# A decoder layer: the second feed-forward's down projection with the activation as stationary operand, and its end with tokens on partitions

## The chip, the core and the metric

The kernel runs on one core of a Trainium2 chip. The metric is the device time of one execution in microseconds, the median of the runs. The engines have the names of the profile: PE (TensorE, products), PEld (its weight loads), DVE (VectorE), ACT (ScalarE), POOL (GpSimd) and SP (SyncE, which issues most DMAs here).

## The reference, cut to what matters

256 tokens with 2048 features get 16 meta tokens in front (272 in all), go through a feed-forward, a mixer (attention beside a short convolution, merged by gates) and a second feed-forward, and a last norm; the meta tokens are dropped. All is float32.

```python
D_MODEL, SEQ, N_META, D_FF = 2048, 256, 16, 5632

def rms_norm(x, g):
    y = x * lax.rsqrt(jnp.mean(x * x, axis=-1, keepdims=True) + RMS_EPS)
    return y * g

def swiglu_ffn(h, w_gu, w_down):
    gate, up = jnp.split(h @ w_gu, 2, axis=-1)
    return (jax.nn.silu(gate) * up) @ w_down

s = jnp.concatenate([meta, x], axis=1)
s = s + 0.5 * swiglu_ffn(rms_norm(s, norm_ffn1), ffn1_w_gu, ffn1_w_down)
...
s = s + merged @ w_out
s = s + 0.5 * swiglu_ffn(rms_norm(s, norm_ffn2), ffn2_w_gu, ffn2_w_down)
s = rms_norm(s, norm_final)
return s[:, N_META:]
```

## The kernel before, in words

The residual stream `s` is kept with features on partitions: `[128, 16 chunks, 272 tokens]`, L142. Every matrix product keeps float32 accuracy by splitting both operands in a high part and a low rest, both of the type float32r (`wh` and `wl` of the weights; the two parts of an activation lie side by side in a tile of class `Act`). A product is then the sum of three: high by high, high weights by low activation, low weights by high activation.

`linear` (L215) makes all the large products. For four output chunks of 128 features it takes four banks of PSUM and goes over the chunks of the contraction. The stationary operand (the one that is loaded into the array) is a 128x128 block of the weights, the moving one the activation with tokens along the row. Where only the 256 real tokens are computed, both parts of the activation fit one bank: `wh` is multiplied with both at once, 512 columns wide (L248), then `wl` with the high part, 256 wide (L252). With 272 tokens, or where `nj` is 1, it is three products of 272 or 256 columns (L250, L251, L252). Weights come in loads of 1 MB into `st` (four buffers, SP's queue), ScalarE casts a block to `wh` (L241), VectorE makes `wl` of it (L242), three buffers each.

Order of the work: what follows a group of outputs (its "evict") waits in the list `pending` and is put in behind the second chunk of the group after it (`EVICT_AT`). Small other work stands in the list `side`; `linear` puts one piece behind the chunks 5, 9 and 13. The framework's planner then orders each engine's instructions and hands out the slots of the pools. The pool `act` has `N_ACT` slots of 4352 bytes per partition, which tiles of several stages share (`xin`, `h1` to `h3`, `m`, `yo` and others).

A feed-forward (`ffn`, L276) is done in two halves of the hidden features, 24 and then 20 chunks: gate and up products, their elementwise part into the activation `m`, and then the down product of that half, which adds to `s` (L313). In the second feed-forward's last half, `after2` (L614) also squares the finished chunk and sums the squares over chunks, multiplies by the last norm's gain, and puts `turn_out` (L631) in `side`: two transposes on TensorE (L635) that turn a chunk to tokens on partitions and two copies into `yo`. The last four output chunks are done one at a time (`nj` = 1, `cut_last`). Behind the last product the sums of squares are turned by products with ones (L624), a root, a reciprocal and a Newton step (`rsqrt`, L203 to L208) give the factor `fr` for each token, `yo` is scaled in five pieces by VectorE and ScalarE (L655, L653), and SP issues five DMAs (L656).

Of the kernel before, what the change touches and what calls it, by code (L numbers as in the profile page):

```python
# [15 lines left out]
P = 128  # L16
D = 2048
# [17 lines left out]
N_ACT = 21  # L35
EVICT_AT = 1
WARM = 6


@with_exitstack  # L40
def decoder_layer(ctx: ExitStack, tc: tile.TileContext, t, out):
# [17 lines left out]
    # the tensor engine's clock comes up while the first loads are under way  # L59
# [21 lines left out]
    NV = 3 * DC + 3 * NH + 1  # L81
    vrows = const.tile([NV, P], F32, name="vrows")
    G_MIX, G_FFN2, G_FIN, G_CONV, G_SUB = 0, DC, 2 * DC, 3 * DC, NV - 1
# [6 lines left out]
    load_gain(G_FIN, t["norm_final"])  # L90
# [68 lines left out]
    def split(act, g, src):  # L159
        """A group's four chunks from float32."""  # L160
        for k in range(2):
            tl, f = act.tiles[2 * g + k], src[:, 2 * k : 2 * k + 2, :]
            nc.scalar.copy(out=tl[:, :, 0, :], in_=f)
            nc.vector.tensor_sub(tl[:, :, 1, :], f, tl[:, :, 0, :].bitcast(F32))

    def gain_split(h, c, gain):
        """gain * s for chunk c, split; the norm's factor for each token is left to the product's outputs."""
        w = h.width
        hi, lo = h.part(c, 0, 0, w), h.part(c, 1, 0, w)
        a = nc.scalar.mul(hi, s[:, c, T - w :], gain)  # L170
        b = nc.vector.scalar_tensor_tensor(
            out=lo, in0=s[:, c, T - w :], scalar=gain, in1=hi.bitcast(F32), op0=ALU.mult, op1=ALU.subtract
        )
        return a.ins, b.ins

    class Norm:
        """Sums of squares over the features, chunk by chunk, and 1 / rms for each token on every partition."""
# [4 lines left out]
        def add(self, c):  # L182
# [4 lines left out]
            nc.scalar.activation(sq[:, self.n0 :], s[:, c, self.n0 :], AF.Square)  # L187
# [12 lines left out]
    def rsqrt(out_, ms, shape, name):  # L200
        """1 / sqrt(ms) with a Newton step."""
# [8 lines left out]
    # ---- the linears: one stream of products; what follows a group of outputs, and any other work, is put  # L210
    # between the products of the groups after it ----
# [3 lines left out]
    def linear(act, chunks, w, k0, c0, t0, t1, name, evict, before=None, side_at=(5, 9, 13), nj=GC):  # L215
# [4 lines left out]
        kb = KB * GC // nj  # L220
        nl = kb if before is not None else LB * kb
        acc = [bank(f"{name}_{j}") for j in range(nj)]
        for b in range(0, len(chunks), kb):
            blk = chunks[b : b + kb]
            r0 = (k0 + blk[0]) * P
            wh = wpool.tile([P, kb, nj * P], F32R, tag="wh", name="wh")
            wl = wpool.tile([P, kb, nj * P], F32R, tag="wl", name="wl")
            m = len(blk)
            if b % nl == 0:
                st = wpool.tile([P, LB * kb, nj * P], F32, tag="st", bufs=ST_BUFS, name="st")  # L230
# [3 lines left out]
                    in_=w[r0 : r0 + ml * P, c0 : c0 + nj * P].rearrange("(c p) f -> p c f", p=P),  # L234
# [8 lines left out]
            for i, c in enumerate(blk):  # L243
                first, last = b + i == 0, b + i == len(chunks) - 1
                for j in range(nj):
                    a, f = acc[j][:, :n], slice(j * P, (j + 1) * P)
                    if shared(n, nj):
# [12 lines left out]
    def shared(n, nj):  # L260
        return 2 * n <= 512 and nj == GC

    def total(ps, n):
        """A product's sum, where its parts have accumulated side by side."""
# [11 lines left out]
    def ffn(h, w_gu, w_down, norm, n0, after, before=None, cut_last=False):  # L276
        """s += 0.5 * swiglu; `after(c)` once chunk c of s is done."""
        n = T - n0
        ng = F // GW
        halves = [list(range(0, (ng + 1) // 2)), list(range((ng + 1) // 2, ng))]  # L280
        allk = list(range(DC))
        for half in halves:
            m = Act("m", len(half) * GC, n)
            for gi, g in enumerate(half):
                sg = wide([P, GC, T], "sg")

                def gate(pg, sg=sg):
                    rstd = norm.rstd[:, n0:]
                    for j in range(GC):
                        gt = tmp.tile([P, T], F32, tag="gt", name="gt")  # L290
                        nc.vector.tensor_mul(gt[:, :n], total(pg[j], n), rstd)
                        sgm = tmp.tile([P, T], F32, tag="sgm", name="sgm")
                        nc.scalar.activation(sgm[:, :n], gt[:, :n], AF.Sigmoid)
                        nc.vector.tensor_mul(gt[:, :n], gt[:, :n], rstd)
                        nc.vector.tensor_mul(sg[:, j, :n], gt[:, :n], sgm[:, :n])

                def up(pu, sg=sg, gi=gi):
                    for j in range(GC):
                        nc.vector.tensor_mul(sg[:, j, :n], total(pu[j], n), sg[:, j, :n])
                    split(m, gi, sg[:, :, :n])  # L300

                linear(h, allk, w_gu, 0, g * GW, 0, n, "pg", gate, before=before)
                before = None
                linear(h, allk, w_gu, 0, F + g * GW, 0, n, "pu", up)
            final = half is halves[-1]
            c = 0
            while c < DC:
                nj = 1 if final and cut_last and c >= DC - GC else GC

                def down(pd, c=c):  # L310
                    for j in range(len(pd)):
                        for k in range(2 if shared(n, len(pd)) else 1):
                            nc.vector.scalar_tensor_tensor(  # L313
                                out=s[:, c + j, n0:], in0=pd[j][:, k * n : (k + 1) * n], scalar=0.5,
                                in1=s[:, c + j, n0:], op0=ALU.mult, op1=ALU.add,
                            )
                        if final:
                            after(c + j)

                linear(m, list(range(len(half) * GC)), w_down, half[0] * GC, c * P, 0, n, "pd", down, nj=nj)  # L320
                c += nj

# [4 lines left out]
    def prep(c):  # L327
# [5 lines left out]
        v = nc.vector.tensor_copy(s[:, c, :], pt[:, :T])  # L333
# [39 lines left out]
    ffn(h1, t["ffn1_w_gu"][0], t["ffn1_w_down"][0], norm1, 0, after1, before=before1)  # L373

# [48 lines left out]
    class Unit:  # L423
        """The attention of one head and one block of 128 queries, in three steps."""
# [106 lines left out]
    # the short convolution  # L531
# [33 lines left out]
    # gates, branches, merge  # L565
# [27 lines left out]
    norm3 = Norm(NMETA, "3")  # L593
    for d in range(D // GW):

        def o_evict(ps, d=d):
            for j in range(GC):
                c = d * GC + j
                for k in range(2):
                    nc.vector.tensor_add(s[:, c, NMETA:], ps[j][:, k * SEQ : (k + 1) * SEQ], s[:, c, NMETA:])  # L600
# [8 lines left out]
    yo = [[apool.tile([P, W2], F32, tag="act", name=f"yo{i}{q}") for q in range(2)] for i in range(2)]  # L609
    norm4 = Norm(NMETA, "4")  # L610

    fsum = []

    def after2(c):  # L614
        sc = s[:, c, NMETA:]
        if c < DC - 1:
            norm4.add(c)
        else:
            sq = tmp.tile([P, SEQ], F32, tag="half", name="fsq")
            nc.scalar.activation(sq, sc, AF.Square)  # L620
            for i in range(2):
                pr = bank(f"pr{i}")
                for k, q in enumerate((norm4.ssq[:, NMETA:], sq)):
                    nc.tensor.matmul(  # L624
                        pr[:, :1], q[:, i * P : (i + 1) * P], ones[:, 0:1], start=k == 0, stop=k == 1
                    )
                fsum.append(pr)
        nc.scalar.mul(sc, sc, col(G_FIN + c))
        side.append(lambda: turn_out(c))

    def turn_out(c):  # L631
        pt = bank("ot")
        c0 = c % NH * P
        for i in range(2):
# [47 lines left out]
```

## Time and profile before

| | before |
|---|---|
| median of 3 runs | 2238.79 us (2238.0 to 2239.01) |
| profiled execution, first to last instruction | 2236.7 us |
| median of the runs less that span | 2.1 us |
| PE, DVE, ACT busy | 2221.1, 1344.9, 1012.5 us |
| mean granted TensorE clock | 0.998 |
| read from HBM | 396.67 MB |
| weights of the down projections | 87 loads of 1 MB and 4 of 256 KB, 5.3 and 2.8 us to landing |

The page gives one execution's span; the runs' times stand beside it, and the profiled execution has no other time of its own. Rows of the timeline read: start, length, engine, line, operation, tile written <- tiles read, and shapes. Groups read: count, then busy us and mean ns of one, then idle time before it with its releaser. TensorE's products overlap their neighbours, so their cost is read from the distance of their starts and not from their lengths.

### The profile page before, as it was taken

The numbers are of one execution on the slowest core, as the hardware profiler recorded it, in microseconds if no ns is written. First come the engines' busy times: TensorE is split into PE (matmuls) and PEld (weight loads), VectorE is DVE, ScalarE is ACT, GpSimd is POOL, SyncE is SP. The second block draws the span as 40 slices with busy tenths as digits, with TensorE's granted clock in tenths as the row PEclk, the third lists the DMA queues.
The fourth block names the chain that finished last, engine by engine and source line by source line (L and its number), as shares of the span: only waits on it lengthen the run. The fifth ranks groups of instructions, "written<-read, shape, count | busy, mean of one in ns | idle before, by whom it ended". The sixth has DMA issues, their size and how long they took to land.

```text
span 2236.7 us, 35912 instructions
## 1 busy us (share of the span) xinstructions
PE 2221.1 (99%) x15068; PEld 2060.5 (92%) x15068; DVE 1344.9 (60%) x1978; ACT 1012.5 (45%) x1357; POOL 5.8 (0%) x16
## 2 busy tenths in 40 slices
PE   9999999999999999999999999999999999999998
PEld 8999999999999999898988888888888888888887
DVE  7555554455555565667766665776666655666665
ACT  6444333334434443445455454555444433545444
POOL 1000000000000000000000000000000000000000
PEclk9999999999999999999999999999999999999999
DMA  6554555555555555444565555555555555555553
GB/s 232 175 182 171 171 178 180 170 173 182 173 170 176 182 170 179 155 139 151 167 191 188 189 187 190 183 193 188 189 190 190 191 192 193 192 188 189 188 174 109
DMA packets 208738, 401.09 MB, mean 179 GB/s; under 512 B 6548, under 2 KB 16992, under 8 KB 208576
## 3 DMA queue, kind: packets, MB, share of 16 engines
q1 hardware_dynamic: 208192, 398.48, 53.7%
q8 instruction: 118, 1.93, 0.4%
q14 instruction: 44, 0.36, 0.0%
q0 software_dynamic: 288, 0.17, 0.0%
q10 hardware_dynamic: 96, 0.14, 0.0%
HBM read 396.67 MB, written 2.10 MB: 178 GB/s over the span
## 4 chain that ended last, share of the span: by engine, by line
PE 99%; ACT 0%; DMA 0%; DVE 0%; ACTq 0%; issue 0%
PE pg L252 8%; PE pd L252 8%; PE pu L252 8%; PE pu L248 7%; PE pg L248 7%; PE pd L248 6%; PE g L248 5%; PE pd L250 4%; PE pd L251 4%; PE pg L250 4%; PE pu L250 4%; PE pg L251 4%; PE pu L251 4%; PE g L252 3%; PE z L248 3%; PE o L248 3%
## 5 line engine op out<-in xcount | busy, mean ns | idle before, releaser
L242 DVE TENSOR_TENSOR wl<-st,wh 128x1024 fp32r<-128x1024 f32 (+1 forms) x754 | 919.7, 1222 | 803.3 <-ACT wh L241 802.4
L241 ACT CAST wh<-st 128x1024 fp32r<-128x1024 f32 (+1 forms) x754 | 792.0, 1051 | 1091.4 <-PE pd L251 155.5
L252 PE MATMUL pd<-m,wl 128*128 128x272 f32 (+1 forms) x1408 | 398.8, 283 | 0.0
L252 PE MATMUL pu<-h,wl 128*128 128x272 f32 (+1 forms) x1408 | 398.0, 283 | 0.0
L252 PE MATMUL pg<-h,wl 128*128 128x272 f32 (+1 forms) x1408 | 396.1, 284 | 0.0
L252 PEld LDWEIGHTS pd<-m,wl 128*128 128x128 f32 x1408 | 265.0, 188 | 0.0
L252 PEld LDWEIGHTS pu<-h,wl 128*128 128x128 f32 x1408 | 264.6, 188 | 0.0
L252 PEld LDWEIGHTS pg<-h,wl 128*128 128x128 f32 x1408 | 264.1, 188 | 0.3 <-DVE wl L242 0.2
L248 PE MATMUL pg<-h,wh 128*128 128x512 f32 x704 | 244.8, 394 | 0.0
L248 PE MATMUL pu<-h,wh 128*128 128x512 f32 x704 | 244.5, 394 | 0.0
L250 PE MATMUL pd<-m,wh 128*128 128x272 f32 (+1 forms) x784 | 226.3, 289 | 0.0
L251 PE MATMUL pd<-m,wh 128*128 128x272 f32 (+1 forms) x784 | 225.0, 287 | 0.0
L248 PE MATMUL pd<-m,wh 128*128 128x512 f32 x624 | 217.6, 395 | 0.0
L250 PE MATMUL pg<-h,wh 128*128 128x272 f32 x704 | 203.4, 290 | 2.0 <-ACT wh L241 2.0
L250 PE MATMUL pu<-h,wh 128*128 128x272 f32 x704 | 203.2, 289 | 0.0
L251 PE MATMUL pu<-h,wh 128*128 128x272 f32 x704 | 202.4, 288 | 0.0
L251 PE MATMUL pg<-h,wh 128*128 128x272 f32 x704 | 202.4, 288 | 0.0
L248 PE MATMUL g<-h,wh 128*128 128x512 f32 x512 | 180.1, 395 | 0.0
L248 PEld LDWEIGHTS pu<-h,wh 128*128 128x128 f32 x704 | 132.0, 188 | 30.7
L248 PEld LDWEIGHTS pg<-h,wh 128*128 128x128 f32 x704 | 132.0, 187 | 30.6
L251 PEld LDWEIGHTS pd<-m,wh 128*128 128x128 f32 x784 | 148.1, 189 | 0.0
L250 PEld LDWEIGHTS pd<-m,wh 128*128 128x128 f32 x784 | 147.5, 188 | 0.0
(211 smaller groups left out, 3336.9 us busy)
## 6 DMA issues: line engine op xcount, KB each, us to landing
st<-in_ffn_w_gu_dram SPq DMA_DIRECT2D x172, 1024.0 KB, 4.9
st<-in_ffn_w_down_dram SPq DMA_DIRECT2D x87, 1024.0 KB, 5.3
st<-in_w_in_dram SPq DMA_DIRECT2D x48, 1024.0 KB, 5.1
st<-in_w_gate_dram SPq DMA_DIRECT2D x32, 1024.0 KB, 5.7
st<-in_w_branch_dram SPq DMA_DIRECT2D x16, 1024.0 KB, 5.3
st<-in_w_out_dram SPq DMA_DIRECT2D x16, 1024.0 KB, 5.3
st<-in_ffn_w_gu_dram SPq DMA_DIRECT2D x8, 512.0 KB, 6.5
xin<-in_x_dram SPq DMA_DIRECT2D x8, 256.0 KB, 7.2
```

The source lines that it names most:

```text
L241: nc.scalar.copy(out=wh[:, :m, :], in_=sw)
L242: nc.vector.tensor_sub(wl[:, :m, :], sw, wh[:, :m, :].bitcast(F32))
L248: nc.tensor.matmul(acc[j][:, : 2 * n], wh[:, i, f], act.both(c, t0, t1), start=first, stop=False)
L250: nc.tensor.matmul(a, wh[:, i, f], act.part(c, 0, t0, t1), start=first, stop=False)
L251: nc.tensor.matmul(a, wh[:, i, f], act.part(c, 1, t0, t1), start=False, stop=False)
L252: nc.tensor.matmul(a, wl[:, i, f], act.part(c, 0, t0, t1), start=False, stop=last)
```

## The change

For the second feed-forward alone, `linear_tok` takes the place of `linear` in the down projection. The activation `m` (128 features by 128 tokens) is loaded into the array, and the weights are the moving operand, 512 features wide. An output bank holds 128 tokens by 512 features; four banks (two token blocks `i` by two feature blocks `q`) make a unit of 1024 features, so the projection has two units for each half of the hidden features. A chunk of the contraction takes 12 products of 512 columns. A load of 1 MB holds two chunks by 1024 features.

The residual stream therefore has to stand with tokens on partitions when the projection's results arrive: behind the output projection of the mixer, `turn` puts four transposes and one ScalarE copy for each four chunks and token block into `side`, into the tiles `sT`. `turn_out`, the sums by products with ones and the single output chunks go. The sum of squares now lies along a row: ScalarE's square accumulates it (`fss`), VectorE multiplies by the last norm's gain, which POOL's queue has brought to all partitions (`gfin`), and `finish(i)` makes the factor, scales, and issues two DMAs for a token block.

In the very last unit (`hold` = 3) the products of token block 1 with the last three chunks are put behind all products of token block 0, so that block 0's end comes before them. `s` moves from a tile of its own into four slots of the pool `act`, which grows from 21 to 25. The first feed-forward computes as before, its loops are written out instead of `ffn`.

```diff
-N_ACT = 21
+N_ACT = 25
 EVICT_AT = 1
 WARM = 6
+HOLD = 3
...
-    s = const.tile([P, DC, T], F32, name="s")
+    sF = [apool.tile([P, GC, T], F32, tag="act", name=f"s{g}") for g in range(DC // GC)]
+
+    def s(c, t0, t1=T):
+        return sF[c // GC][:, c % GC, t0:t1]
...
+    def linear_tok(act, chunks, w, k0, c0, name, evict, side_at=(5, 9, 13), hold=0):
+        acc = [[bank(f"{name}{i}{q}") for q in range(2)] for i in range(2)]
+        nk = len(chunks)
+        held = []
+        def products(b, i, q, wh, wl):
+            ps, tok = acc[i][q], slice(i * P, (i + 1) * P)
+            c, first, last = chunks[b], b == 0, b == nk - 1
+            nc.tensor.matmul(ps, act.part(c, 0, tok.start, tok.stop), wh[:, q, :], start=first, stop=False)
+            nc.tensor.matmul(ps, act.part(c, 1, tok.start, tok.stop), wh[:, q, :], start=False, stop=False)
+            nc.tensor.matmul(ps, act.part(c, 0, tok.start, tok.stop), wl[:, q, :], start=False, stop=last)
+        for b, c in enumerate(chunks):
+            if b % 2 == 0:
+                st = wpool.tile([P, 2, 2, GW], F32, tag="st", bufs=ST_BUFS, name="st")
+                r0 = (k0 + c) * P
+                nc.sync.dma_start(
+                    out=st,
+                    in_=w[r0 : r0 + 2 * P, c0 : c0 + 2 * GW].rearrange("(c p) (q f) -> p c q f", p=P, f=GW),
+                )
+            sw = st[:, b % 2]
+            wh = wpool.tile([P, 2, GW], F32R, tag="wh", name="wh")
+            wl = wpool.tile([P, 2, GW], F32R, tag="wl", name="wl")
+            nc.scalar.copy(out=wh, in_=sw)
+            nc.vector.tensor_sub(wl, sw, wh.bitcast(F32))
+            for i in range(2):
+                if i and b >= nk - hold:
+                    held.append((b, wh, wl))
+                    continue
+                for q in range(2):
+                    products(b, i, q, wh, wl)
+            if b == EVICT_AT:
+                flush()
+            if b in side_at and side:
+                side.pop(0)()
+        flush()
+        if not hold:
+            pending.append(lambda: [evict(i, q, acc[i][q]) for q in range(2) for i in range(2)])
+            return
+        for q in range(2):
+            evict(0, q, acc[0][q])
+        for q in range(2):
+            for b, wh, wl in held:
+                products(b, 1, q, wh, wl)
+            evict(1, q, acc[1][q])
...
+    sT = [[apool.tile([P, W2], F32, tag="act", name=f"sT{i}{q}") for q in range(2)] for i in range(2)]
+    def turn(d, i):
+        pt = bank("st_ps")
+        for j in range(GC):
+            nc.tensor.transpose(pt[:, j * P : (j + 1) * P], s(d * GC + j, NMETA + i * P, NMETA + (i + 1) * P), ident)
+        nc.scalar.copy(out=sT[i][d // 2][:, d % 2 * GW : (d % 2 + 1) * GW], in_=pt)
     for d in range(D // GW):
         def o_evict(ps, d=d):
             for j in range(GC):
                 c = d * GC + j
                 for k in range(2):
-                    nc.vector.tensor_add(s[:, c, NMETA:], ps[j][:, k * SEQ : (k + 1) * SEQ], s[:, c, NMETA:])
+                    nc.vector.tensor_add(s(c, NMETA), ps[j][:, k * SEQ : (k + 1) * SEQ], s(c, NMETA))
                 gain_split(h3, c, col(G_FFN2 + c))
                 norm3.add(c)
             if d == D // GW - 1:
-                side.append(norm3.end)
+                side.insert(0, norm3.end)
+            side.extend(lambda d=d, i=i: turn(d, i) for i in range(2))
         linear(mg, allk, w_out, 0, d * GW, 0, SEQ, "o", o_evict)
...
+    gfin = [apool.tile([P, W2], F32, tag="act", name=f"gfin{q}") for q in range(2)]
+    fss = const.tile([P, 2, 2 * 2], F32, name="fss")
+    def finish(i):
+        ssq = const.tile([P, 1], F32, name=f"fssq{i}")
+        nc.vector.tensor_reduce(out=ssq, in_=fss[:, i, :], axis=AX.X, op=ALU.add)
+        fms = const.tile([P, 1], F32, name=f"fms{i}")
+        nc.vector.tensor_scalar(fms, ssq, 1.0 / D, EPS, op0=ALU.mult, op1=ALU.add)
+        fr = const.tile([P, 1], F32, name=f"fr{i}")
+        rsqrt(fr, fms, [P, 1], f"f{i}")
+        for q in range(2):
+            y = sT[i][q]
+            if q:
+                nc.scalar.mul(y, y, fr)
+            else:
+                nc.vector.tensor_scalar_mul(y, y, fr)
+            nc.sync.dma_start(out=out[i * P : (i + 1) * P, q * W2 : (q + 1) * W2], in_=y)
+    w_gu, w_down = t["ffn2_w_gu"][0], t["ffn2_w_down"][0]
+    for half in halves:
+        m = gate_up(h3, half, w_gu, norm3, NMETA)
+        final = half is halves[-1]
+        if final:
+            for q in range(2):
+                nc.gpsimd.dma_start(
+                    out=gfin[q],
+                    in_=t["norm_final"][q * W2 : (q + 1) * W2].rearrange("(o d) -> o d", o=1).to_broadcast([P, W2]),
+                )
+        for u in range(2):
+            def down(i, q, ps, u=u, final=final):
+                fs = slice(q * GW, (q + 1) * GW)
+                v = sT[i][u][:, fs]
+                nc.vector.scalar_tensor_tensor(out=v, in0=ps, scalar=0.5, in1=v, op0=ALU.mult, op1=ALU.add)
+                if final:
+                    k = u * 2 + q
+                    sq = wide([P, GW], "fsq")
+                    nc.scalar.activation(sq, v, AF.Square, accum_out=fss[:, i, k : k + 1])
+                    nc.vector.tensor_mul(v, v, gfin[u][:, fs])
+                    if k == 3:
+                        finish(i)
+            linear_tok(
+                m, list(range(len(half) * GC)), w_down, half[0] * GC, u * W2, "pd", down, hold=HOLD if final and u else 0
+            )
```

The lines of `after2`, `turn_out` and what followed them (L609 to L656) go; they stand in the listing above.

More of the change, by code (lines that the diff above doesn't have):

```diff
@@ L89, in decoder_layer @@
     load_gain(G_FFN2, t["norm_ffn2"][0])
-    load_gain(G_FIN, t["norm_final"])
     nc.gpsimd.dma_start(
@@ L213, in decoder_layer, with linear @@
     side = []
-    def linear(act, chunks, w, k0, c0, t0, t1, name, evict, before=None, side_at=(5, 9, 13), nj=GC):
+    def linear(act, chunks, w, k0, c0, t0, t1, name, evict, before=None, side_at=(5, 9, 13)):
         n = t1 - t0
-        kb = KB * GC // nj
+        kb = KB
         nl = kb if before is not None else LB * kb
-        acc = [bank(f"{name}_{j}") for j in range(nj)]
+        acc = [bank(f"{name}_{j}") for j in range(GC)]
         for b in range(0, len(chunks), kb):
@@ L274, in flush @@
             pending.pop(0)()
-    def ffn(h, w_gu, w_down, norm, n0, after, before=None, cut_last=False):
-        n = T - n0
[L279 to L321, printed above, removed]
@@ new lines, in decoder_layer, with gate_up, gate, up @@
+    ng = F // GW
+    halves = [list(range(0, (ng + 1) // 2)), list(range((ng + 1) // 2, ng))]
+    def gate_up(h, half, w_gu, norm, n0, before=None):
+        n = T - n0
+        m = Act("m", len(half) * GC, n)
+        for gi, g in enumerate(half):
+            sg = wide([P, GC, T], "sg")
+            def gate(pg, sg=sg):
+                rstd = norm.rstd[:, n0:]
+                for j in range(GC):
+                    gt = tmp.tile([P, T], F32, tag="gt", name="gt")
+                    nc.vector.tensor_mul(gt[:, :n], total(pg[j], n), rstd)
+                    sgm = tmp.tile([P, T], F32, tag="sgm", name="sgm")
+                    nc.scalar.activation(sgm[:, :n], gt[:, :n], AF.Sigmoid)
+                    nc.vector.tensor_mul(gt[:, :n], gt[:, :n], rstd)
+                    nc.vector.tensor_mul(sg[:, j, :n], gt[:, :n], sgm[:, :n])
+            def up(pu, sg=sg, gi=gi):
+                for j in range(GC):
+                    nc.vector.tensor_mul(sg[:, j, :n], total(pu[j], n), sg[:, j, :n])
+                split(m, gi, sg[:, :, :n])
+            linear(h, list(range(DC)), w_gu, 0, g * GW, 0, n, "pg", gate, before=before)
+            before = None
+            linear(h, list(range(DC)), w_gu, 0, F + g * GW, 0, n, "pu", up)
+        return m
@@ L371, in after1, with down @@
             side.append(norm2.end)
-    ffn(h1, t["ffn1_w_gu"][0], t["ffn1_w_down"][0], norm1, 0, after1, before=before1)
+    for half in halves:
+        m = gate_up(h1, half, t["ffn1_w_gu"][0], norm1, 0, before1 if half is halves[0] else None)
+        for c in range(0, DC, GC):
+            def down(pd, c=c, final=half is halves[-1]):
+                for j in range(GC):
+                    nc.vector.scalar_tensor_tensor(
+                        out=s(c + j, 0), in0=pd[j][:, :T], scalar=0.5, in1=s(c + j, 0), op0=ALU.mult, op1=ALU.add
+                    )
+                    if final:
+                        after1(c + j)
+            linear(m, list(range(len(half) * GC)), t["ffn1_w_down"][0], half[0] * GC, c * P, 0, T, "pd", down)
     w_in, w_gate, w_out = t["w_in"][0], t["w_gate"][0], t["w_out"][0]
@@ L631, in turn_out @@
[L631 to L634, printed above, removed]
-            nc.tensor.transpose(pt[:, i * P : (i + 1) * P], s[:, c, NMETA + i * P : NMETA + (i + 1) * P], ident)
-        for i in range(2):
-            nc.vector.tensor_copy(yo[i][c // NH][:, c0 : c0 + P], pt[:, i * P : (i + 1) * P])
-    ffn(h3, t["ffn2_w_gu"][0], t["ffn2_w_down"][0], norm3, NMETA, after2, cut_last=True)
-    flush()
-    fms = const.tile([P, 2], F32, name="fms")
-    for i in range(2):
-        nc.vector.tensor_scalar(fms[:, i : i + 1], fsum[i][:, :1], 1.0 / D, EPS, op0=ALU.mult, op1=ALU.add)
```

61 lines of the change are left out of this document (15 added, 46 removed).

## The prediction

> **What bounds the kernel now.** I read the page's busy shares and its chain first, then the windows of the stage that is changed, then single products in the timeline, and last the chain through the end.
>
> ```profile
> span 2236.7 us, 35912 instructions
> PE 2221.1 (99%) x15068; PEld 2060.5 (92%) x15068; DVE 1344.9 (60%) x1978; ACT 1012.5 (45%) x1357; POOL 5.8 (0%) x16
> ...
> PEclk9999999999999999999999999999999999999999
> ...
> PE 99%; ACT 0%; DMA 0%; DVE 0%; ACTq 0%; issue 0%
> ```
>
> The chain is 99% TensorE: what the change is worth is the time it takes out of TensorE's stream, plus what it takes off the end. The windows (us; then busy time and count of PE, PEld, DVE, ACT, POOL; granted clock, DMA share, GB/s) show the first half of the second down projection, and the end behind the last product:
>
> ```profile
> 1755.00:1885.00 130.00, 130.00 (x753) 113.65 (x751) 67.51 (x77) 50.77 (x51) 0.00 (x0) 1.00 0.58 194
> ...
> 2224.63:2236.70 12.07, 1.32 (x10) 0.97 (x9) 3.59 (x13) 4.60 (x6) 0.00 (x0) 0.66 0.45 174
> ```
>
> In the projection TensorE never rests; VectorE is busy 67.5 of 130 us, ScalarE 50.8, the DMA engines 58%. So the stage is its number of products times the spacing of their starts. The two parts of the down projection are bounded by these starts (the second row is the first product behind the first part, the last one the last product of all):
>
> ```profile
> 1753.61 0.39 PE L248 MATMUL pd<-m,wh 128*128 128x512 f32 x1
> ...
> 1886.73 0.39 PE L248 MATMUL pg<-h,wh 128*128 128x512 f32 x1
> ...
> 2108.60 0.39 PE L248 MATMUL pd<-m,wh 128*128 128x512 f32 x1
> ...
> 2193.52 0.28 PE L250 MATMUL pd<-m,wh 128*128 128x256 f32 x1
> ...
> 2224.35 0.28 PE L252 MATMUL pd<-m,wl 128*128 128x256 f32 x1
> ```
>
> Part one: 24 rows of chunks by 16 output chunks, each a 512-wide and a 256-wide product: 384 pairs in 133.12 us, 346.7 ns a pair. Part two: 20 by 12 pairs, then from 2193.52 on 20 by 4 triples of 256-wide products (the last four output chunks are done singly). The bare 256-wide spacing, and for comparison the 272-wide one of the first feed-forward:
>
> ```profile
> 2219.79 0.28 PE L250 MATMUL pd<-m,wh 128*128 128x256 f32 x1
> ...
> 2220.15 0.28 PE L250 MATMUL pd<-m,wh 128*128 128x256 f32 x1
> ```
>
> ```profile
> 400.11 0.29 PE L250 MATMUL pd<-m,wh 128*128 128x272 f32 x1
> ...
> 401.24 0.29 PE L250 MATMUL pd<-m,wh 128*128 128x272 f32 x1
> ```
>
> Three 256-wide products in 0.36 us are 120 ns each; nine 272-wide in 1.13 us are 125.6. With 120 for the 256-wide half of a pair, the 512-wide half is 346.7 - 120 = 226.7 ns. From 256 to 512 columns that is 106.7 ns for 256 more columns, 0.4167 ns a column, and 13.3 ns a product that do not depend on its width. The 272-wide row gives 125.6 - 113.3 = 12.3 by the same slope, near enough. This fixed 13 ns is what a change to fewer, wider products can save.
>
> **Term 1, the products.** Columns streamed stay the same: a weight chunk of 512 features against 256 tokens was 4 x (512 + 256) = 3072 columns in 8 products, and becomes 2 token blocks x 3 x 512 = 3072 columns in 6. In all, before: 624 pairs x 346.7 = 216.3 us, and 240 single products x 120 = 28.8: 245.1 us, 1488 products. After: 44 chunks x 2 halves of the features x 2 token blocks x 2 banks x 3 = 1056 products x 226.7 = 239.4 us. Saved: 5.7 us, which is also 432 products x 13.3. The trace has no 512-wide product behind another, so I bound it: 225.6 ns (12.3 fixed) gives 238.2 us and 6.9 saved; the chain's rounded steps reach
>
> ```profile
> 2150.33 0.24 PE pd L248
> ```
>
> 240 ns, which would be 253.4 us, 8.3 more than before. I take 226.7: it comes from 384 pairs. That three products in a row accumulate in one bank needs no price: the triples above do so at 120 ns.
>
> Here the Trainium skill speaks against the gain. TensorE: Matmul & The Clock Gate, Back-to-back issue gap, gives a warm gap of N/2.4 + 2.5 ns: by that the 432 products saved are worth an estimated 1.1 us and not 5.7. The 256-wide row at 120 ns, where the rule gives an estimated 109.2, disagrees, and the measurement decides; the rule stands among the rivals.
>
> **Term 2, the transposes.** 32 go (`turn_out`, L635, during the last down linears), 32 come (`turn`, four at a time, during the output projection and the first gate linear).
>
> ```profile
> 2206.71 0.28 PE L252 MATMUL pd<-m,wl 128*128 128x256 f32 x1
> 2206.83 0.38 PE L635 MATMUL ot<-ident,s 128*128 128x128 f32 x2
> ...
> 2207.16 0.28 PE L251 MATMUL pd<-m,wh 128*128 128x256 f32 x1
> ```
>
> From L252 to L251, two steps that take 0.24 without them, is 0.45: 0.21 us a pair. Part two was 115.87 us to the end of its spacing (2108.60 to 2224.47) against 83.2 + 28.8 = 112.0 by Term 1, so its 15 pairs cost 3.9 with all that hangs on them; 16 pairs at 0.21 are 3.4. I take 3.6 after (3.4 to 4.1): 0.3 saved. Would `turn` make TensorE wait for `s`? Its place, chunk 5 of the next linear, is where `norm3.end` stands now behind the last output group:
>
> ```profile
> 1489.99 0.75 DVE L600 TENSOR_TENSOR s<-o,s 128x256 f32<-128x256 f32 x2
> ```
>
> ```profile
> 1495.26 0.59 PE L194 MATMUL ssq_ps<-ssq,ones 128*128 128x256 f32 x2
> ```
>
> The last add to `s` ends at 1490.74 and the place comes at 1495.26: 4.5 us to spare. Its copy out of the bank goes to ScalarE, which idles 1.72 us before each cast there, and a copy of this form takes 591 ns; were that cover gone, 8 x 0.6 = 4.7 us.
>
> ```profile
> L412 ACT COPY vN<-pv 128x512 f32<-128x512 f32 x4 | 2.2, 591 | 0.0
> ```
>
> ```profile
> 1459.29 1.06 ACT L241 CAST wh<-st 128x1024 fp32r<-128x1024 f32 x1 [1.72 <-PE o L248]
> ```
>
> At nothing go: the weight loads (44 of 1 MB for 43 and 4 quarter ones, SP's queue not full at 58%); casts and splits, 88 of the same size, a chunk's cast of 1.06 us (row above) and split of 1.23 (row below) under 12 x 226.7 = 2.72 us of products, three buffers; in the last three chunks, which run at half that, up to 2 x (2.28 - 1.36) = 1.8 us if the buffers were empty. `norm_final`'s broadcast goes on POOL's queue, with nothing behind it, 1 MB in a stage of 100 us.
>
> ```profile
> 1460.38 1.23 DVE L242 TENSOR_TENSOR wl<-st,wh 128x1024 fp32r<-128x1024 f32 x1 [1.55 <-ACT wh L241]
> ```
>
> **Term 3, the end.** The chain (start, length, what) behind the last product:
>
> ```profile
> 2224.51 0.13 PE pd L252
> 2224.67 0.44 DVE s L313
> 2225.12 0.42 ACT fsq L620
> 2225.57 0.51 ACT s L628
> 2226.10 1.28 ACT L203
> 2227.39 0.21 ACT rsaf L203
> ...
> 2228.62 1.15 ACT yo L653
> 2229.77 1.04 ACTq L678
> ```
>
> ```profile
> 2229.00 3.13 SPq L656 DMA_DIRECT2D out_dram<-yo  x5
> ```
>
> ```profile
> GB/s 0 0 0 0 0 33 0 0 0 0 0 0 0 0 0 0 0 0 0 74 262 393 434 393 393 402 401 410 434 393 205 0 0 0 0 0 0 0 0 0
> ```
>
> Before: the product ends at 2224.64, scaling runs from 2228.62 to 2230.81, the 2 MB leave between 2229.5 and 2235.2 (slices of 0.5 us from 2220), the span ends at 2236.7: 12.06 us. After, the last three chunks' products for token block 1 are held back: 18 x 0.227 = 4.1 us of TensorE, during which block 0 is finished, with the table load (1.28) and its 1 MB. For block 1 what is left behind the last product goes by these rows:
>
> ```profile
> L242 DVE TENSOR_TENSOR wl<-st,wh 128x512 fp32r<-128x512 f32 x4 | 2.7, 683 | 0.0
> ```
>
> ```profile
> L241 ACT CAST wh<-st 128x512 fp32r<-128x512 f32 x4 | 2.5, 622 | 2.9 <-PE pd L248 1.8 <-PE pd L251 1.2
> ```
>
> ```profile
> L479 ACT ACTIVATION_READ_ACCUMULATOR junk<-oN 128x1 f32 x16 | 3.0, 187 | 0.0
> ```
>
> ```profile
> L653 ACT ACTIVATE yo<-yo,fr 128x1024 f32<-128x1024 f32 x2 | 2.2, 1141 | 1.0 <-DVE fr L208 1.0
> L655 DVE TENSOR_SCALAR yo<-yo,fr 128x1024 f32<-128x1024 f32 x1 | 0.7, 747 | 0.0
> ```
>
> Add 0.68, square 0.62 + 0.19, sum and mean about 0.4, root 0.24, and the 1.0 between 2227.6 and 2228.62: 3.2 us if nothing is in the way, then 1.14 to scale: 4.3. VectorE may be in the way: from the end of block 0's first bank, 0.7 us before the held products, it has 4 adds and 4 gain multiplies (8 x 0.68), 14 small steps at about 0.18 and two scalings of 0.75, 9.5 us, so it cannot end before 4.7 us behind the last product; with its waits for ScalarE up to 6.2, no better than before. I take 5.3 for the slower scaling; VectorE's half is out 0.4 us earlier. From that issue: 0.5 to start, 1 MB at 400 GB/s 2.6, and 1.5 from the last byte to the end as before (2235.2 to 2236.7): 4.6. So 5.3 - 0.4 + 4.6 = 9.5 us (8.6 to 10.9): 2.5 saved (1.2 to 3.5).
>
> **Sum.** 5.7 + 0.3 + 2.5 = 8.5 us off the profiled span of 2236.7 gives 2228.2; the median of the runs, 2238.79, lies 2.1 above that span, so 2230.3 us. Smallest to largest terms (5.7 - 2 for a wait of the splits, -0.2, 1.2; and 6.9, 0.5, 3.5): 2227.9 to 2234.1.
>
> **Rivals.** What a measurement here can tell from no change is 0.2%, 4.5 us: below 2234.3 is faster, above 2243.3 slower.
>
> (a) The 13.3 ns do not belong to a product but go with columns. By columns alone a pair is 346.7/768 = 0.451 ns a column, and 540,672 columns cost 244.1 us in any shape: 1.0 saved, with Term 3 3.5, so 2235.3: the same. Against: 256 columns alone cost 0.469 each and not 0.451. The gap of the Trainium skill quoted in Term 1 (TensorE: Matmul & The Clock Gate, Back-to-back issue gap) would save an estimated 1.1 us of products too. The change then does not do what it says. 0.10.
>
> ```profile
> L252 PEld LDWEIGHTS pd<-m,wl 128*128 128x128 f32 x1408 | 265.0, 188 | 0.0
> ```
>
> (b) Slower: a 512-wide product behind another, each with its own weight load, starts later than 226.7 ns. Place: both parts of the down projection. It decides from (245.1 + 0.3 + 2.5)/1056 = 234.8 ns on; at 240 ns the products lose 8.3, less 2.8: 2244.3. For it: the chain's 0.24 steps. Against: they stand mostly by transposes, the weight load, 188 ns in the row above, lies well inside, and the pairs average 226.7. A lower granted clock would do the same; against it 1.00 in the windows at a stream already 99% busy. 0.08.
>
> (c) The slots. `s`, `sT` and `gfin` now lie in the pool of 25: in the second feed-forward 8 of `h3`, 4 of `sT`, 12 of `m` are 24. If `gfin`, which waits for no data, takes the spare ones early, an eviction waits for a slot and TensorE for a linear's part: half of one (16 x 1.39 = 22.2 us) is 11 us, 2241, and more is slower. 0.07, most of it slower.
>
> (d) Only the end fails (scaling 6.2 and no more): 2232, within the forecast.
>
> **How the numbers follow.** Forecast 0.75 at 2230.3, own range 2227.5 to 2234.3. With (a) 0.10, (b) 0.08, (c) 0.07: faster 0.76, same 0.11, slower 0.13. Some 0.7 lies in the forecast's own range; to hold 8 in 10 it reaches over (a): 2227.2 to 2238.0.
>
> **What would show it.** Right: products of `pd` 226 to 227 ns apart throughout, 1056 of them, both parts about 130.6 and 108.8 us with no transposes in them; 0.42 us for each `turn` and no idle TensorE there; behind the last product 9 to 10 us, no table load in it, and only half of the output's bytes. Wrong: a spacing of 233 ns or more; TensorE idle for `wl` in the last chunks; an add for block 1 that stands behind block 0's steps on VectorE until 6 us behind the last product; evictions that wait for slots between 1500 and 1750 us.

## The result, and the profile after

The changed kernel takes 2242.13 us (median of 21 runs, 2240.98 to 2242.87) against 2238.93 (21 runs, 2237.91 to 2239.58): ratio 1.0014, interval 1.0008 to 1.0021. It is slower by 3.2 us, where 8.5 us less were forecast. The page of the changed kernel, shares and chain:

```profile
span 2239.2 us, 34942 instructions
PE 2223.7 (99%) x14628; PEld 2043.6 (91%) x14628; DVE 1328.9 (59%) x1900; ACT 1007.2 (45%) x1348; POOL 6.4 (0%) x17
...
PE 99%; ACT 0%; DVE 0%; POOL 0%; issue 0%; POOLq 0%
```

TensorE still sets the time, with 440 instructions fewer and 2.6 us more busy. The stages from the output projection on are bounded by these starts, first of the changed kernel (output projection, second linear of gate and up, down part one, gate and up of the second half, down part two, last product), then the two of before that the prediction does not show:

```profile
1397.39 0.39 PE L251 MATMUL o<-mg,wh 128*128 128x512 f32 x1
...
1513.68 0.40 PE L251 MATMUL pu<-h,wh 128*128 128x512 f32 x1
...
1762.43 0.40 PE L287 MATMUL pd<-wh,m 128*128 128x512 f32 x1
...
1893.02 0.39 PE L251 MATMUL pg<-h,wh 128*128 128x512 f32 x1
...
2119.14 0.40 PE L287 MATMUL pd<-wh,m 128*128 128x512 f32 x1
...
2227.74 0.39 PE L289 MATMUL pd<-wl,m 128*128 128x512 f32 x1
```

```profile
1398.19 0.39 PE L248 MATMUL o<-mg,wh 128*128 128x512 f32 x1
...
1509.56 0.39 PE L248 MATMUL pu<-h,wh 128*128 128x512 f32 x1
```

| stage | before, us | after, us | difference |
|---|---|---|---|
| all ahead of the output projection | 1398.19 | 1397.39 | -0.80 |
| output projection and first gate linear | 111.37 | 116.29 | +4.92 |
| rest of gate and up, first half | 244.05 | 248.75 | +4.70 |
| down, part one | 133.12 | 130.59 | -2.53 |
| gate and up, second half | 221.87 | 226.12 | +4.25 |
| down, part two, to the end of its spacing | 115.87 | 108.83 | -7.04 |
| the end | 12.23 | 11.23 | -1.00 |
| profiled span | 2236.7 | 2239.2 | +2.5 |

The first row is scatter: in the twelve profiles of this document whose products keep their order (all but e5 to e7), the output projection starts between 1397.34 and 1399.08 us, with either kernel. From that start to the end it is 838.5 us before and 841.8 after, 3.3 more, like the medians.

The down projection got as much faster as forecast. What ate it lies mostly in the gate and up products, which the change does not touch. The same windows of the two kernels, first before, then after (columns as in the prediction):

```profile
1600.00:1700.00 100.00, 100.00 (x579) 87.46 (x578) 66.22 (x101) 49.16 (x69) 0.00 (x0) 1.00 0.55 190
1980.00:2080.00 100.00, 100.00 (x579) 87.44 (x578) 63.29 (x90) 47.81 (x64) 0.00 (x0) 1.00 0.55 190
```

```profile
1600.00:1700.00 100.00, 100.00 (x568) 86.67 (x567) 65.22 (x100) 49.10 (x71) 0.00 (x0) 1.00 0.54 188
1980.00:2080.00 100.00, 100.00 (x568) 86.67 (x568) 65.20 (x98) 49.25 (x70) 0.00 (x0) 1.00 0.55 186
```

Same clock (1.00), no idle time, much the same work on the other engines, and 568 products in 100 us instead of 579. A pair of a 512-wide and a 256-wide product takes 353.3 ns instead of 346.7: the first half's 704 pairs in 248.75 us, the second's 640 in 226.12. TensorE waits for nothing; the row of products itself has a second, slower rhythm.

### The profile page after: what moved, and what is told of

Same layout as the page of the kernel before. It is cut to its first block, busy times and chain, and to the rows that moved or that the text cites. A ratio compares the mean times of both kernels' runs of the same rounds, so it can differ in the third digit from the quotient of the medians.

```text
span 2239.2 us, 34942 instructions
## 1 busy us (share of the span) xinstructions
PE 2223.7 (99%) x14628; PEld 2043.6 (91%) x14628; DVE 1328.9 (59%) x1900; ACT 1007.2 (45%) x1348; POOL 6.4 (0%) x17
## 4 chain that ended last, share of the span: by engine, by line
PE 99%; ACT 0%; DVE 0%; POOL 0%; issue 0%; POOLq 0%
PE pg L255 8%; PE pu L255 8%; PE pu L251 7%; PE pg L251 7%; PE g L251 5%; PE pg L253 4%; PE pd L255 4%; PE pu L253 4%; PE pd L253 4%; PE pg L254 4%; PE pu L254 4%; PE pd L254 4%; PE pd L288 3%; PE pd L289 3%; PE pd L287 3%; PE g L255 3%
## 5 line engine op out<-in xcount | busy, mean ns | idle before, releaser
L245 DVE TENSOR_TENSOR wl<-st,wh 128x1024 fp32r<-128x1024 f32 x664 | 810.7, 1223 | 714.8 <-ACT wh L244 714.3
L244 ACT CAST wh<-st 128x1024 fp32r<-128x1024 f32 x664 | 697.1, 1050 | 965.1 <-PE pd L254 146.9
L251 PE MATMUL pg<-h,wh 128*128 128x512 f32 x704 | 249.6, 399 | 0.0
L251 PE MATMUL pu<-h,wh 128*128 128x512 f32 x704 | 249.2, 399 | 0.0
L255 PE MATMUL pd<-m,wl 128*128 128x272 f32 x704 | 203.0, 288 | 0.0
L253 PE MATMUL pd<-m,wh 128*128 128x272 f32 x704 | 202.9, 288 | 0.0
L254 PE MATMUL pd<-m,wh 128*128 128x272 f32 x704 | 202.4, 288 | 0.0
L303 DVE TENSOR_TENSOR wl<-st,wh 128x1024 fp32r<-128x1024 f32 x88 | 107.6, 1224 | 114.8 <-ACT wh L302 114.7
L302 ACT CAST wh<-st 128x1024 fp32r<-128x1024 f32 x88 | 92.8, 1054 | 137.4 <-PE pd L288 129.4
L255 PE MATMUL g<-h,wl 128*128 128x256 f32 x512 | 143.4, 280 | 0.0
L288 PE MATMUL pd<-wh,m 128*128 128x512 f32 x352 | 137.0, 389 | 0.0
```

The source lines that it names most:

```text
L244: nc.scalar.copy(out=wh[:, :m, :], in_=sw)
L245: nc.vector.tensor_sub(wl[:, :m, :], sw, wh[:, :m, :].bitcast(F32))
L251: nc.tensor.matmul(acc[j][:, : 2 * n], wh[:, i, f], act.both(c, t0, t1), start=first, stop=False)
L253: nc.tensor.matmul(a, wh[:, i, f], act.part(c, 0, t0, t1), start=first, stop=False)
L254: nc.tensor.matmul(a, wh[:, i, f], act.part(c, 1, t0, t1), start=False, stop=False)
L255: nc.tensor.matmul(a, wl[:, i, f], act.part(c, 0, t0, t1), start=False, stop=last)
```

## The experiments

The theory after the comparison (R): the pairs have two rhythms; whatever is put between them can switch the rhythm, and it then stays until the next break. The rival (P): tiles lie in other slots, and reading them is slower.

**e1: the norm's product behind the last transposes.**

```diff
-            if d == D // GW - 1:
-                side.insert(0, norm3.end)
             side.extend(lambda d=d, i=i: turn(d, i) for i in range(2))
+            if d == D // GW - 1:
+                side.append(norm3.end)
```

> The changed kernel with one order swapped: the third norm's end (a plain product of 256 columns with ones, behind it a root) comes behind the last two groups of transposes instead of ahead of them. Nothing else moves. Theory R (rhythm): the pairs of a 512-wide and a 256-wide product run in one of two rhythms, 346.7 or 353.3 ns, which the last thing put between them sets and which stays until the next one; four transposes leave the slow one, the plain product leaves the fast one. Then the gate and up products of the first half run at 346.7: some 710 pairs x 6.67 ns = 4.7 us less than the changed kernel, about 2237.4 us, or 9 us less if the fast rhythm lasts through the 512-wide run into the second half. Rival P (place): the pairs are slower because tiles lie in other slots of the pool; the slots are as in the changed kernel, so no change, 2242 us.

Measured: 2237.75 us (2236.47 to 2238.37), 4.4 less than the changed kernel. Its two windows:

```profile
1600.00:1700.00 100.00, 100.00 (x578) 87.37 (x578) 66.84 (x104) 50.38 (x72) 0.00 (x0) 1.00 0.57 189
1980.00:2080.00 100.00, 100.00 (x569) 86.71 (x568) 64.90 (x97) 49.02 (x69) 0.00 (x0) 1.00 0.57 187
```

The first half is back at 346.7 ns though the edit adds no tile, so P as stated falls (the slots themselves are not in the traces). The second half is slow again from its first pairs on, behind a fast first half: the run of 512-wide products leads to the slow rhythm by itself.

**e2: a plain product in the second half.** `plain` multiplies `ones` by 256 columns of `mask`; it is put in `side` ahead of the second half's `gate_up`.

```diff
+            side.append(plain)
         m = gate_up(h3, half, w_gu, norm3, NMETA)
```

> As e1_norm_last, and one more plain product of 256 columns (ones by the mask, its result not read) behind the sixth chunk of the second half's first gate products. Theory R: the run of 512-wide products leaves the slow rhythm too, and the plain product ends it there: 640 pairs x 6.67 ns = 4.3 us more than e1 gains, 9 us in all, about 2233 us. If e1 has gained the second half already, the same as e1 within 0.5 us. Rival P: 2242 us, or 0.3 more for the added product.

Measured: 2238.04 us (2236.86 to 2238.46), as e1. The pairs stayed at 353.3 behind the product:

```profile
1980.00:2080.00 100.00, 100.00 (x568) 86.74 (x567) 65.51 (x98) 48.95 (x70) 0.00 (x0) 1.00 0.57 185
```

The same kind of break that ended the slow rhythm in the first half did not end it here.

**e3: the kernel before with the transposes.** `turn` with its eight groups of four transposes is put into the kernel before, its copies go to scratch.

> The kernel before, with the eight groups of four transposes and their ScalarE copies put in where the changed kernel has them; the copies go to scratch and are not used, slots and products are those of before. Theory R: the pairs run at 353.3 ns from the first group in the output projection until the first transposes of the end: about 2000 pairs x 6.67 ns = 13 us (some less where the third norm's product comes between), and 3.4 us for the transposes: about 2255 us. Rival P: 3.4 us for the transposes, 2242.4 us.

Measured: 2243.14 us (2241.87 to 2243.65), 4.1 more than before. That is the transposes (3.5 us by their size below) and little else: of the stretches behind the eight groups, one ran at 353 ns, the others at 346.7. So transposes as such do not lead to the slow rhythm, though in the changed kernel all eight groups did.

**e4: nothing held back.** `HOLD = 0`, with a `flush()` at the end.

> The changed kernel with no products held back: all four banks of the last unit end together. Theory H (the held products hide the end of token block 0): VectorE and ScalarE begin 2 to 4 us later against the last product, the table load and 2 MB of output are on the path: 2.5 to 4 us slower, 2245 us. Rival: VectorE's own 9.5 us of steps set the end in either order, less than 1 us slower.

Measured: 2244.0 us (2243.05 to 2244.95), 1.9 more than the changed kernel: between the two expectations. Holding products back works, for less than was thought.

**e5 and e6: the widths not alternated.** In `linear`, the four 512-wide products of a chunk come first, then the four 256-wide ones, in the kernel before (e5) and in the changed one (e6).

```diff
-                for j in range(GC):
-                    (512-wide of j, then 256-wide of j)
+                for part in range(2):
+                    for j in range(GC):
+                        (512-wide of j if part is 0, else 256-wide of j)
```

> The kernel before, with the products of a chunk in another order wherever a 512-wide and a 256-wide product share a bank: the four 512-wide ones first, then the four 256-wide ones. Same products. Theory R (rhythm): its pairs in the output projection and the second feed-forward are in the fast rhythm already, so only the query, gate and short convolution linears of the mixer, whose pairs take some 350 ns, can gain: up to 900 pairs x 3.5 ns = 3 us; 2236 to 2239 us. Rival S (each change of width costs some ns, in either order): two changes for eight products in place of eight, so all 2800 pairs gain a few ns: 2230 us or less.

> The changed kernel with the same order of products as e5_before_grouped. Theory R: no alternation, so no slow rhythm: the 10.5 us that the changed kernel's slow pairs cost (1570 pairs x 6.67 ns) go, and what e5 gains comes on top: 2229 to 2232 us, 6 to 8 us below e5, which is what the prediction's terms gave less the 1.5 us by which the end fell short. Rival S: as e5, 2235 us or less, but by the same amount as e5 gains. Rival P (slots): no gain beyond that of e5.

Measured: e5 2247.38 us (2247.23 to 2248.45), ratio 1.0039 (1.0025 to 1.0053); e6 2239.44 (2238.35 to 2240.05), ratio 1.0001 (0.9993 to 1.001). Both expectations for e5 missed: this order runs between the two rhythms, 573 products in 100 us, and in e6 a little slower, 572:

```profile
1980.00:2080.00 100.00, 100.00 (x573) 87.57 (x572) 65.35 (x98) 48.32 (x70) 0.00 (x0) 1.00 0.57 186
1980.00:2080.00 100.00, 100.00 (x572) 87.39 (x571) 64.70 (x97) 48.80 (x70) 0.00 (x0) 1.00 0.57 185
```

By the stage of 704 pairs (246.40 and 246.99 us) a pair takes 350.0 ns in e5 and 350.8 in e6. The order costs the kernel before 8 us and gives the changed one 2.7, so the 2229 to 2232 us expected for e6 missed as well. The 6 to 8 us between the two came: with almost the same pace of gate and up on both sides the changed kernel is 7.9 us faster.

**e7: the root's table early.** e6, and one root on ScalarE in the last unit:

```diff
+                    if i + k == 0:
+                        pre = const.tile([P, 1], F32, name="pre")
+                        nc.scalar.activation(pre, fss[:, 0, 0:1], AF.Sqrt)
```

> As e6_after_grouped, and ScalarE takes one root of a number that is there early in the last unit, so that the table of roots (1.28 us) is loaded before the end. Theory: the load stood on the end's chain (ScalarE at 2227.70, between block 1's first square and block 0's root): 1.0 to 1.5 us less than e6. Rival: VectorE's steps set the end, less than 0.5 us.

Measured: 2238.58 us (2237.61 to 2239.16), 0.9 below e6, too little for the intervals to part them. In the two profiles the way from the start of the last product to the end is 10.8 instead of 11.5 us: 0.7, between the two expectations.

**e8: ten breaks of ten widths.** As e1, with a plain product of another width in each linear of the second half.

> As e1_norm_last, and in each of the ten gate and up linears of the second half one plain product behind the sixth chunk, 272, 256, 224, 192, 160, 128, 96, 64, 32 and 16 columns wide (results not read). Theory R, in which the time at which the row is taken up again picks the rhythm: some widths lead to 346.7 ns, others to 353.3, with the same tiles in the same slots. Rival P (slots): 353.3 throughout the second half. Rival K (the kind of the break picks it): plain products lead to one and the same rhythm, whatever their width.

A single run, 2238.55 us. The windows behind 272, 256, 224, 192 and 160 columns, each 18 us long:

```profile
1900.00:1918.00 18.00, 18.00 (x106) 15.73 (x105) 11.42 (x19) 9.65 (x15) 0.00 (x0) 1.00 0.54 176
1922.00:1940.00 18.00, 18.00 (x106) 15.87 (x105) 11.20 (x17) 8.63 (x13) 0.00 (x0) 1.00 0.56 183
1944.00:1962.00 18.00, 18.00 (x104) 15.62 (x103) 11.09 (x18) 8.20 (x13) 0.00 (x0) 1.00 0.56 180
1967.00:1985.00 18.00, 18.00 (x106) 15.87 (x105) 11.31 (x16) 8.63 (x12) 0.00 (x0) 1.00 0.57 192
1990.00:2008.00 18.00, 18.00 (x104) 15.60 (x103) 11.19 (x19) 8.79 (x14) 0.00 (x0) 1.00 0.55 176
```

Fast, fast, slow, fast, slow, and slow behind all narrower ones (by the spacing of the starts 346.7 or 353.3). One kind of break, the same tiles, both rhythms: neither the kind of the break nor the slots alone decide. That its length does is not shown by e8 alone, since each width stands at another place and not all behind the same rhythm; at one place, behind the same slow pairs, 256 columns (e2) and 272 (e9 below) are to be compared.

**e9 and e10: the break that helps.** e1 with the 272-wide product at the first place of the second half (e9), and with e7's early root besides (e10).

> As e1_norm_last, and one plain product, 272 columns wide, behind the sixth chunk of the second half's first gate products; e8 showed this width lead into the fast rhythm there. Theory R: nothing breaks the row between it and the down projection, so all ten linears run at 346.7 ns: 630 pairs x 6.67 = 4.2 us less than e1, 0.3 us for the product itself: 2233.8 us (2233 to 2235), faster than both kernels. Rival: the widths of e8 worked because they came often, or by chance of that run: as e2, 2238 us.

> As e9_plain272, with the early root of e7 besides. If the two gains are independent, 0.9 us less than e9: 2232.9 us.

Measured: e9 2233.56 us (2232.74 to 2234.37), ratio to the kernel before 0.9977 (0.9967 to 0.9986); e10 2231.55 (2230.82 to 2232.22), ratio 0.9966 (0.9954 to 0.9978). Both beat both kernels, e10 by 7.3 us the one of before. The second half of e9, now at the pace of before, where e2 stayed slow with a product 16 columns narrower at the same place (it also reads `mask` from another column on):

```profile
1980.00:2080.00 100.00, 100.00 (x579) 87.43 (x578) 64.70 (x95) 49.48 (x69) 0.00 (x0) 1.00 0.58 190
```

e10 gained 2.0 over e9 and not 0.9. The rest lies in the output projection: behind the same transposes its pairs run at 346.7, in e9 at 353.3. Up to there the two programs differ in addresses alone: e10's constant `pre` moves all weight and activation tiles by 32 bytes. (Addresses are read from the built programs here and below; no trace shows them.)

**e11: one product of 160 columns in the kernel before.**

> The kernel before, and one plain product of 160 columns (not read) behind the third norm's end, in the first gate products of the second feed-forward; e8 showed this width lead from the fast rhythm into the slow one. Theory R: everything from there to the first transposes of the end runs at 353.3 ns, gate, up and the down projection too: 1830 pairs x 6.67 = 12.2 us, 2251 us, from one product of 0.2 us in a kernel whose weights, slots and order are otherwise those of before. If this width at this place leads back to the fast rhythm: 2239.5 us. Rival (the slow pairs need the changed kernel's slots or its 512-wide run): 2239.5 us.

Measured: 2239.47 us (2238.49 to 2240.46): the fast rhythm held, no effect. A width that led from fast to slow in e8 did not do so here.

**e12 and e13: 32 bytes.** By the tile addresses of the built programs, weights and activations lie at 32 modulo 64 bytes in the changed kernel, e1 and e9, and at 0 in the kernel before, e3 and e10.

```diff
+    room = const.tile([P, 8], F32, name="room")
+    nc.vector.memset(room, 0.0)
```

> The changed kernel with one unused constant of 32 bytes per partition (and its memset), which moves every tile behind it from 32 to 0 modulo 64 bytes, where they lie in the kernel before. Theory A (offset): at 0 the transposes leave the fast rhythm, as in e3 and e10: the output projection and the first half's gate and up products gain 920 pairs x 6.67 ns = 6.1 us, while the second half stays slow behind the 512-wide run, as in e10 before its plain product: 2236 us. Theory R alone (only the time of the break counts): 2242 us.

> e3_before_turns with the same 32 bytes, which move its tiles from 0 to 32 modulo 64. Theory A: the transposes now leave the slow rhythm as in the changed kernel, until the first transposes of the end: some 2000 pairs x 6.67 ns = 13 us above e3's 2243.1, 2256 us. Theory R alone: 2243 us.

Measured: e12 2235.91 us (2234.88 to 2236.51), 6.2 below the changed kernel, as the offset's theory gave, and faster than the kernel before, ratio 0.9986 (0.9977 to 0.9995). e13 2242.41 (2241.51 to 2243.55), as e3: the theory's other half fell. In e13 the stretches of the output projection alternate. Fourteen pairs behind the first group of transposes and fourteen behind the second:

```profile
1430.37 0.39 PE L251 MATMUL o<-mg,wh 128*128 128x512 f32 x1
...
1435.32 0.40 PE L251 MATMUL o<-mg,wh 128*128 128x512 f32 x1
...
1436.47 0.39 PE L251 MATMUL o<-mg,wh 128*128 128x512 f32 x1
...
1441.32 0.39 PE L251 MATMUL o<-mg,wh 128*128 128x512 f32 x1
```

4.95 us, slow; 4.85, fast. So 32 bytes change which rhythm a break leads to, but no rule "0 is fast, 32 is slow" holds. What keeps the two rhythms, and what picks one, stays open.

## Why the prediction was wrong, point by point

**The step that failed is the sum: it has no term for the products that the change leaves alone.** Terms 1 and 2 price the run of 512-wide products and the transposes at their own time, and the pairs of the output projection, of gate and of up are kept at 346.7 ns, at nothing and without a reason. They ran at 353.3: 209 pairs behind transposes up to 1513.68 us, 704 in the first half and 640 in the second, 1553 x 6.67 ns = 10.3 us. In the first half the slow rhythm comes from the last transposes, at 1510 us, and lasts to 1762. The second half is slow behind the 512-wide run; it is so in e1 and e12 too, where the first half is fast.

A sign of it stood in the rows of before: 15 pairs of transposes cost 3.9 us where 15 x 0.21 are 3.2, and the prediction put the rest down as "all that hangs on them". Behind some of those transposes the pairs already ran slowly for the few us until the next break. Here are 14 pairs behind one and 14 behind the next:

```profile
2145.22 0.40 PE L248 MATMUL pd<-m,wh 128*128 128x512 f32 x1
...
2150.16 0.40 PE L248 MATMUL pd<-m,wh 128*128 128x512 f32 x1
...
2151.09 0.40 PE L248 MATMUL pd<-m,wh 128*128 128x512 f32 x1
...
2155.95 0.39 PE L248 MATMUL pd<-m,wh 128*128 128x512 f32 x1
```

They take 4.94 and 4.86 us, 353 and 347 ns a pair; 53 such slow pairs cost 0.35 of the 3.9 us. Rival (b) had seen the 0.24 us steps and looked for them in the down projection alone; no rival had the stages that the change leaves alone.

**Term 2, the transposes themselves,** came out at its size. Four of them and the taking up again, here behind the first output group:

```profile
1427.78 0.28 PE L255 MATMUL o<-mg,wl 128*128 128x256 f32 x1
1427.89 0.60 PE L644 MATMUL st_ps<-ident,s 128*128 128x128 f32 x4
1428.25 0.48 PE L251 MATMUL o<-mg,wh 128*128 128x512 f32 x1
...
1428.68 0.40 PE L251 MATMUL o<-mg,wh 128*128 128x512 f32 x1
```

From 1427.89 to 1428.25 it is 0.36 us, and the pair behind takes 0.43 where the slow rhythm has 0.353: 0.44 us a group, eight times 3.5; summed were 3.6. The table gives the same: 4.92 us less 209 slow pairs (1.39) is 3.53. Against the 3.87 of before 0.3 us was saved, as forecast. No wait for `s`, as said.

**Term 1 was right to a tenth.** Three products of 512 columns in 0.68 us, 226.7 each:

```profile
2221.17 0.39 PE L287 MATMUL pd<-wh,m 128*128 128x512 f32 x1
...
2221.85 0.39 PE L287 MATMUL pd<-wh,m 128*128 128x512 f32 x1
```

Part one took 130.59 us (forecast 130.6), part two 108.83 (108.8). Without the transposes of before (3.87) the saving is 2.53 + 7.04 - 3.87 = 5.7 us, the number of the sum. The Trainium skill's gap (TensorE: Matmul & The Clock Gate, Back-to-back issue gap), there for a product by itself, gives an estimated 215.8 ns for 512 columns; the trace has 226.7. Rival (a), by which the products save 1.0 us, falls: they saved 5.7.

**Term 3 was too large:** 1.0 us saved, forecast 2.5 and at least 1.2. The chain of the changed kernel from the last unit on:

```profile
2226.96 0.72 ACT fsq L701 x2
...
2227.70 1.28 ACT L206
...
2229.00 0.21 ACT rsaf L206
...
2229.97 0.60 DVE sT L702
...
2230.67 1.15 ACT sT L677
2231.82 0.10 ACT rsaf L206
...
2232.91 1.15 ACT sT L677
```

The last product ends at about 2228.1; block 1 is scaled from 2232.91 to 2234.06, 5.9 us behind it, inside the forecast's 4.7 to 6.2 but at its late end. Block 0 was not done when the held products were: VectorE's gain multiplies came ahead of block 0's sum, ScalarE took block 1's first square ahead of the table load, so block 0 is scaled only at 2230.67 and its bytes leave with block 1's:

```profile
GB/s 0 0 0 0 0 0 0 0 0 0 0 0 0 0 172 410 410 402 393 393 426 393 393 418 385 0 0 0 0 0 0 0 0 0 0 0 0 0 0 0
```

In slices of 0.5 us from 2225, the whole 2 MB go out between 2232.0 and 2237.5, behind the last product as in the kernel before. That only half of the output's bytes would be left behind the last product is what failed here; e4 and e7 priced what holding back (1.9) and the table load (0.7) are worth.

**The sum without the rhythm** is 5.7 + 0.3 + 1.0 = 7.0 us. e12 gives the same: from the start of the output projection to the end it takes 835.8 us against 838.5 before, and its second half still has 4.25 us of slow pairs. With 10.3 us of slow pairs, 7.0 saved become the 3.3 lost. The 7.9 us of e5 against e6 are another sum: the grouped order also slows the down projection of before (part one 134.40 us instead of 133.12; 2.1 us over all its 624 pairs), and gate and up take 1.1 us more in e6 than in e5. Rival (c) falls: in the list of waits of the changed kernel from 1500 to 1760 us no eviction waits for a slot.

By the prediction's own bounds (2234.3 and 2243.3 us) the result is "the same", at a chance of 0.11; the interval of 21 runs is narrower than the 0.2% that it allowed for and shows a small loss. Neither that chance nor the 0.13 for slower held a case in which a change outside its own stage costs time.

## What to carry to other kernels

Where TensorE is the bound and never waits, compare the spacing of starts (or products per 100 us) in every stage, also in those that a change does not touch: 2% there is more than the change. Before a change of this kind is given up, try it with its breaks moved, lengthened by one small product, or its tiles moved by 32 bytes; here that turned 3.2 us slower into 7.3 us faster (e10, 0.7 of it by the early root). And price a break in a dense row, or a run of other products, by what follows it until the next break, and not by its own length alone.

## What the runs showed of the hardware that was not expected

Pairs of a 512-wide and a 256-wide product, each with its own weight load, run at 346.7 or 353.3 ns at the same granted clock of 1.00, and keep the rhythm for 250 us (1510.78 to 1762.08 in the changed kernel). At one place a plain product of 272 columns led to the fast one (e9) and one of 256 did not (e2); 224 and 160 led away from it in e8, but 160 did not in e11; and 32 bytes of offset changed the outcome behind the same instructions (e12). The run of equal 512-wide products kept 226.7 ns in every profile of the changed kernel, and in the eight of them with alternating widths the pairs behind it began at 353.3. Four 512-wide ahead of four 256-wide products ran at 350.0 to 350.8 ns a pair (e5, e6).
